# A row-wise infinity norm: new widths for the loads of the last eight tiles

## The chip, the cores and the metric

The kernel runs on one core of one Trainium2 chip. The metric is the device time of one execution in microseconds (us). All executions told of here are in the fast state, with a granted clock of 1.0; no other cores run.

Some terms. A partition is one of the 128 rows of the on-chip memory. VectorE is the engine that runs the reduces here; SyncE issues the loads (`nc.sync`), ScalarE's queue most of the stores (`nc.scalar`). A semaphore is a counter that a finished load raises and that a waiting instruction watches; a load has landed when its semaphore has reached its full count.

## The reference

```python
x = np.random.randn(8192, 8192).astype(np.float32)
def reference(x):
    return np.linalg.norm(x, ord=np.inf, axis=1)
```

For each row of 8192 numbers the result is the largest absolute value. The input is 268.4 MB, the output 32 KB, and each number is looked at once.

## The kernel before

Each of 128 partitions holds two rows in a tile of 16384 columns (64 KB a partition, 8 MB in all). Three such buffers are in use. The first 24 tiles, "the bulk", are loaded whole and reduced whole; the last eight, "the tail", are loaded in the pieces that `TAIL` lists, each row by itself, and each piece is reduced as it lands, so that little work is left after the last byte.

```python
TAIL = (
    [[8192]] * 8
    + [[4096, 4096]] * 5
    + [[2048] * 4] * 2
    + [[2048, 2048, 2048, 1024, 512, 512]]
)
# ... (cut: start_first_load_early, which moves the first load to the program's head; shapes)
    def absmax(o, i):
        nc.vector.reduce_max(out=o, in_=i, axis=X, apply_absolute_value=True)

    for a in range(A):              # bulk
        for n in range(G):
            t = sbuf.tile([P, B * cols + 16], F32, tag="t")
            nc.sync.dma_start(out=t[:, : B * cols], in_=x_b[a, n])
            absmax(r_bulk[:, a, n * B : (n + 1) * B],
                   t[:, : B * cols].rearrange("p (b c) -> p b c", b=B))
    nc.scalar.dma_start(out=out_b, in_=r_bulk[:])

    for i in range(0, n_tail, B):   # tail
        t = sbuf.tile([P, B * cols + 16], F32, tag="t")
        for j in range(B):
            r = i + j; at = j * cols; last = r == n_tail - 1
            for k, w in enumerate(TAIL[r]):
                nc.sync.dma_start(out=t[:, at : at + w], in_=x_t[i // B][:, at : at + w])
                if last and k == k_last - 1:
                    absmax(r_tail[:, : n_tail - 1], part[:])
                    nc.scalar.dma_start(out=out_t[:, : n_tail - 1], in_=r_tail[:, : n_tail - 1])
                    absmax(r_fin[:], t[:, at : B * cols + k_last - 1])
                elif last:          # partial results stand right behind the row
                    absmax(t[:, B * cols + k : B * cols + k + 1], t[:, at : at + w])
                else:
                    absmax(part[:, r, k : k + 1], t[:, at : at + w])
                at += w
    nc.sync.dma_start(out=out_t[:, n_tail - 1 :], in_=r_fin[:])
```

The last reduce of the last row reads the last piece together with the partial results behind it, so no further reduce is needed.

## Time and profile before

The time was 629.22 us (median of three executions, 629.04 to 629.8). The profiled one took 629.1, of which the profile's span holds 627.3.

| what | before |
|---|---|
| DMA share and throughput, 60 to 470 us | 1.00, 433 GB/s |
| VectorE busy | 552.7 us (88%) |
| last load lands | 622.73 us |
| last reduce ends | 624.96 us |
| result's store lands | 626.40 us |

The landing times come from the trace's record of each load, from its issue to the last increment of its semaphore. From the page of the kernel before: the span, the busy engines, groups of reduces (count, then busy time and mean ns of one, then idle time of VectorE ahead of them and what ended it), and the store of the bulk results (count, size, us from issue to landing).

```profile
span 627.3 us, 196 instructions
...
DVE 552.7 (88%) x58; POOL 0.2 (0%) x4
...
L81 DVE TENSOR_REDUCE r_bulk<-t 128x2 f32<-128x16384 f32 x24 | 413.3, 17220 | 69.7 <-DMA t<-in_x_dram 69.7
L81 DVE TENSOR_REDUCE part<-t 128x1 f32<-128x4096 f32 (+2 forms) x26 | 130.0, 5067 | 1.3 <-DMA t<-in_x_dram 1.3
L81 DVE TENSOR_REDUCE t<-t 128x1 f32<-128x2048 f32 (+2 forms) x5 | 8.6, 1746 | 0.3 <-DMA t<-in_x_dram 0.3
...
out_dram<-r_bulk ACTq DMA_DIRECT2D x1, 24.0 KB, 57.9
```

In the bulk VectorE waits 69.7 us for loads, and this costs nothing, since the loads are the limit. In the tail it waits 1.3 + 0.3 us.

From the table of stretches of the kernel before (stretch, its length, busy time of VectorE and of GpSimd, clock, DMA share, GB/s):

```profile
60.00:470.00 410.00, 364.90 (x22) 0.00 (x0) 1.00 1.00 433
...
600.00:622.00 22.00, 21.63 (x11) 0.00 (x0) 1.00 1.00 418
```

The DMA engines are full, nearly to the end. The Trainium skill, "DMA: Bandwidth & Descriptors", section "Specifications", gives 435 GB/s as the fabric's ceiling; this trace's 433 agrees with it. By these two figures another arrangement of the same bytes could shorten the middle by half a per cent at most.

From the timeline of the kernel before, the drain (start, duration, engine, instruction, count, and in brackets the idle time before it and what ended it):

```profile
617.75 2.29 DVE L81 TENSOR_REDUCE t<-t 128x1 f32<-128x2048 f32 x1 [0.15 <-DMA t<-in_x_dram]
620.23 4.00 DVE L81 TENSOR_REDUCE t<-t 128x1 f32<-128x2048 f32 x3 [0.19 <-DMA t<-in_x_dram]
624.26 0.69 DVE L81 TENSOR_REDUCE r_fin<-t 128x1 f32<-128x517 f32 x1
624.98 0.35 SPq L117 DMA_DIRECT2D out_dram<-r_fin  x1
```

The chain of waits of the kernel before ends in the same place:

```profile
603.13 17.07 DMA t<-in_x_dram
620.20 0.02 issue
620.23 2.55 DVE t L81 x2
...
624.26 0.69 DVE r_fin L81
```

At 620.20 the last load of 2048 columns lands and VectorE, which waited for it, starts its reduce. From there VectorE is never idle, and the end is fixed: the reduces of 2048, 1024, 512 and 512 columns one after the other. The last load lands meanwhile, at 622.73, and waits its turn. Between the last landing and VectorE's end lie 2.23 us, called the lag from here on.

From SyncE's queue of the kernel before, what it waited for (us in total, times, longest):

```profile
SPq L100 <- DMA out_dram<-r_bulk: 23.2, 1, 23.2
```

The program has eight completion semaphores for DMAs, used in turn, so a load waits for the DMA eight before it. One of those is the slow store of the bulk results.

### The profile page before, as it was taken

The numbers are of one execution on the slowest core, as the hardware profiler recorded it, in microseconds if no ns is written. First come the engines' busy times: TensorE is split into PE (matmuls) and PEld (weight loads), VectorE is DVE, ScalarE is ACT, GpSimd is POOL, SyncE is SP. The second block draws the span as 40 slices with busy tenths as digits, with TensorE's granted clock in tenths as the row PEclk, the third lists the DMA queues.
The fourth block names the chain that finished last, engine by engine and source line by source line (L and its number), as shares of the span: only waits on it lengthen the run. The fifth ranks groups of instructions, "written<-read, shape, count | busy, mean of one in ns | idle before, by whom it ended". The sixth has DMA issues, their size and how long they took to land.

```text
span 627.3 us, 196 instructions
## 1 busy us (share of the span) xinstructions
DVE 552.7 (88%) x58; POOL 0.2 (0%) x4
## 2 busy tenths in 40 slices
DVE  0588988889988889888898888998889999999998
POOL 0000000000000000000000000000000000000000
DMA  9999999999999999999999999999999999999996
GB/s 401 468 401 464 405 460 410 455 414 451 418 451 418 451 418 447 422 447 422 447 422 447 422 447 422 447 422 443 426 420 428 425 433 435 426 429 427 427 425 274
DMA packets 9138, 268.49 MB, mean 428 GB/s; under 512 B 1968, under 2 KB 1968, under 8 KB 2352
## 3 DMA queue, kind: packets, MB, share of 16 engines
q1 hardware_dynamic: 8208, 268.44, 99.2%
q10 hardware_dynamic: 928, 0.03, 0.1%
q14 instruction: 2, 0.02, 0.0%
HBM read 268.44 MB, written 0.03 MB: 428 GB/s over the span
## 4 chain that ended last, share of the span: by engine, by line
DMA 64%; DVE 30%; another core or an unknown queue 4%; issue 1%; SPq 0%
DMA t<-in_x_dram 64%; DVE r_bulk L81 24%; DVE part L81 5%; DVE t L81 1%; SPq L100 0%; DVE r_fin L81 0%
## 5 line engine op out<-in xcount | busy, mean ns | idle before, releaser
L81 DVE TENSOR_REDUCE r_bulk<-t 128x2 f32<-128x16384 f32 x24 | 413.3, 17220 | 69.7 <-DMA t<-in_x_dram 69.7
L81 DVE TENSOR_REDUCE part<-t 128x1 f32<-128x4096 f32 (+2 forms) x26 | 130.0, 5067 | 1.3 <-DMA t<-in_x_dram 1.3
L81 DVE TENSOR_REDUCE t<-t 128x1 f32<-128x2048 f32 (+2 forms) x5 | 8.6, 1746 | 0.3 <-DMA t<-in_x_dram 0.3
L78 DVE MEMSET part<- 128x60 f32 x1 | 0.1, 108 | 0.9 <-PEq L133 0.9
L81 DVE TENSOR_REDUCE r_fin<-t 128x1 f32<-128x517 f32 x1 | 0.7, 691 | 0.0
L81 DVE TENSOR_REDUCE r_tail<-part 128x15 f32<-128x60 f32 x1 | 0.2, 216 | 0.0
L133 POOL MEMSET const-bfloat16-1.0<- 128x1 bf16 x1 | 0.1, 101 | 0.0
L133 POOL MEMSET const-uint8-127<- 128x1 uint8 x1 | 0.1, 101 | 0.0
L133 POOL MEMSET const-float32-0.0<- 128x1 f32 x1 | 0.1, 98 | 0.2 <-issue 0.2
L133 POOL MEMSET const-float32-1.0<- 128x1 f32 x1 | 0.1, 98 | 0.0
## 6 DMA issues: line engine op xcount, KB each, us to landing
t<-in_x_dram SPq DMA_DIRECT2D x8, 4096.0 KB, 37.0
t<-in_x_dram SPq DMA_DIRECT2D x10, 2048.0 KB, 30.4
t<-in_x_dram SPq DMA_DIRECT2D x11, 1024.0 KB, 24.6
t<-in_x_dram SPq DMA_DIRECT2D x1, 512.0 KB, 15.9
t<-in_x_dram SPq DMA_DIRECT2D x2, 256.0 KB, 13.2
t<-in_x_dram SPq DMA_DIRECT2D x24, 40.7
out_dram<-r_bulk ACTq DMA_DIRECT2D x1, 24.0 KB, 57.9
out_dram<-r_tail ACTq DMA_DIRECT2D x1, 7.5 KB, 5.6
```

Of the source, the lines that this page charges most:

```text
L78: nc.vector.memset(part[:], 0.0)
L81: nc.vector.reduce_max(out=o, in_=i, axis=X, apply_absolute_value=True)
L133: nc = _bacc.Bacc("TRN2", target_bir_lowering=False, num_devices=1)
```

## The change

A reduce costs about 1.04 ns a column and a load about 1.18 ns, a ratio of 0.88. If each load has 0.88 of the width of the one before, each reduce is done about when the next load lands. The change writes the last two tiles about so, from 3968 down to 1024 columns with one step up (1024 to 1152). The change also lets a load cross from one row of a tile to the next; a reduce does not cross, so seven loads get two reduces. Loads in the tail go from 32 to 31, reduces of loaded columns from 32 to 38.

```diff
-TAIL = (
-    [[8192]] * 8
-    + [[4096, 4096]] * 5
-    + [[2048] * 4] * 2
-    + [[2048, 2048, 2048, 1024, 512, 512]]
-)
+TAIL = [
+    [2944, 13440],
+    [4096, 12288],
+    [11520, 4864],
+    [7680, 8704],
+    [6528, 3328, 6528],
+    [4864, 4096, 3328, 4096],
+    [3968, 3584, 3328, 2944, 2560],
+    [2432, 2176, 1920, 1664, 1536, 1280, 1152, 1024, 1152, 1024, 1024],
+]
+def segments(loads, cols):          # (load, row, column, width), cut at row ends
+    ...
@@ tail loop (cut) @@
+    for i, loads in enumerate(TAIL):
+        t = sbuf.tile([P, W + PAD], F32, tag="t")
+        for j, w in enumerate(loads):
+            nc.sync.dma_start(out=t[:, at : at + w], in_=x_t[i][:, at : at + w])
+            at += w
+            for _, b, c, n in [s for s in todo if s[0] == j]:
+                ...                 # one absmax for each segment, results as before
```

The store of the first 15 tail rows now stands in the program right after the last reduce of row 15, no longer behind the last load. In the kernel before, too, it was issued at that point (at 615.44 us).

More of the change, by code (lines that the diff above doesn't have):

```diff
@@ L13 @@
 X = mybir.AxisListType.X
-TAIL = (
-    [[8192]] * 8
-    + [[4096, 4096]] * 5
-    + [[2048] * 4] * 2
-    + [[2048, 2048, 2048, 1024, 512, 512]]
-)
+TAIL = [
[9 more added lines that the diff above has]
+def segments(loads, cols):
+    out, at = [], 0
+    for i, w in enumerate(loads):
+        end = at + w
+        while at < end:
+            r = at // cols
+            to = min(end, (r + 1) * cols)
+            out.append((i, r, at - r * cols, to - at))
+            at = to
+    return out
 def start_first_load_early(nc):
@@ L51 @@
     BUFS: int = 3,
+    PAD: int = 16,
 ):
@@ L55 @@
     rows, cols = x.shape
-    n_tail = len(TAIL)
-    assert n_tail % B == 0
+    W = B * cols
+    n_tail = B * len(TAIL)
     n_bulk_rows = rows // P - n_tail
@@ L70 @@
     outp = ctx.enter_context(tc.tile_pool(name="outp", bufs=1))
-    k_last = len(TAIL[-1])
+    segs = [segments(loads, cols) for loads in TAIL]
+    count = {}
+    for i, s in enumerate(segs):
+        for _, r, _, _ in s:
+            count[i * B + r] = count.get(i * B + r, 0) + 1
+    n_last = count[n_tail - 1]
+    k_max = max(count[r] for r in range(n_tail - 1))
+    assert n_last - 1 <= PAD
     r_bulk = outp.tile([P, A, G * B], F32)
@@ L75 @@
     r_fin = outp.tile([P, 1], F32)
-    k_max = max(len(r) for r in TAIL[:-1])
     part = outp.tile([P, n_tail - 1, k_max], F32)
@@ L84 @@
         for n in range(G):
-            t = sbuf.tile([P, B * cols + 16], F32, tag="t")
-            nc.sync.dma_start(out=t[:, : B * cols], in_=x_b[a, n])
+            t = sbuf.tile([P, W + PAD], F32, tag="t")
+            nc.sync.dma_start(out=t[:, :W], in_=x_b[a, n])
             absmax(
                 r_bulk[:, a, n * B : (n + 1) * B],
-                t[:, : B * cols].rearrange("p (b c) -> p b c", b=B),
+                t[:, :W].rearrange("p (b c) -> p b c", b=B),
             )
     nc.scalar.dma_start(out=out_b, in_=r_bulk[:])
-    for i in range(0, n_tail, B):
-        t = sbuf.tile([P, B * cols + 16], F32, tag="t")
-        for j in range(B):
-            r = i + j
-            at = j * cols
-            last = r == n_tail - 1
-            for k, w in enumerate(TAIL[r]):
-                nc.sync.dma_start(
-                    out=t[:, at : at + w], in_=x_t[i // B][:, at : at + w]
-                )
-                if last and k == k_last - 1:
-                    absmax(r_tail[:, : n_tail - 1], part[:])
-                    nc.scalar.dma_start(
-                        out=out_t[:, : n_tail - 1], in_=r_tail[:, : n_tail - 1]
-                    )
-                    absmax(r_fin[:], t[:, at : B * cols + k_last - 1])
-                elif last:
-                    absmax(
-                        t[:, B * cols + k : B * cols + k + 1], t[:, at : at + w]
-                    )
-                else:
-                    absmax(part[:, r, k : k + 1], t[:, at : at + w])
-                at += w
@@ new lines @@
+    seen = {}
+    for i, loads in enumerate(TAIL):
+        t = sbuf.tile([P, W + PAD], F32, tag="t")
+        todo = segs[i]
+        at = 0
+        for j, w in enumerate(loads):
+            nc.sync.dma_start(out=t[:, at : at + w], in_=x_t[i][:, at : at + w])
+            at += w
+            for _, b, c, n in [s for s in todo if s[0] == j]:
+                r = i * B + b
+                k = seen.get(r, 0)
+                seen[r] = k + 1
+                lo = b * cols + c
+                if r < n_tail - 1:
+                    absmax(part[:, r, k : k + 1], t[:, lo : lo + n])
+                    if r == n_tail - 2 and k == count[r] - 1:
+                        absmax(r_tail[:, : n_tail - 1], part[:])
+                        nc.scalar.dma_start(
+                            out=out_t[:, : n_tail - 1], in_=r_tail[:, : n_tail - 1]
+                        )
+                elif k < n_last - 1:
+                    absmax(t[:, W + k : W + k + 1], t[:, lo : lo + n])
+                else:
+                    absmax(r_fin[:], t[:, lo : W + n_last - 1])
```

## The prediction

> **What bounds the kernel.** The loads. From 60 to 470 us the stretch table shows a DMA share of 1.00 and 433 GB/s; the Trainium skill, "DMA: Bandwidth & Descriptors", section "Specifications", gives 435 GB/s as the fabric ceiling, so nothing is left there, and the 268.4 MB stay the same. VectorE is 88% busy (page, part 1). In the bulk a 16384-column tile lands every 19.34 us and its reduce takes 17.22 us (timeline); some 20 us of loads are outstanding at each issue, so the queue never runs dry.
>
> Open are only the start (first landing 22.0 us, untouched) and the drain. In the trace the last load lands at 622.73 us, the last reduce ends at 624.95, its store lands at 626.40, and the span ends at 627.32 (the measured time adds 1.9). Only the 2.2 us between last landing and VectorE's end are for sale.
>
> **Why 2.2 us.** Reduces cost about 1.04 ns a column plus 0.06 us (starts 8.59 us apart for 8192 columns, 2.20 for 2048, 1.13 for 1024); loads 1.18 ns a column. VectorE enters the tail 17.2 us behind and gains 2.2 us a tile, so it has little to spare: it idles 1.67 us in the tail (timeline: 0.38, 0.56, 0.38, 0.15, 0.19). The last wait is at 620.20, for a load of 2048; its reduce (2.2 us) then stands in front of 1024, 512 and 512, which land within 2.5 us. A step of a half is too steep for rates that differ by 12%.
>
> **What the change does.** Loads 32 -> 31, reduces 32 -> 38 (row boundaries split seven loads): +0.4 us of VectorE work. Each load is about 0.88 of the one before, so a reduce ends about when the next load lands, and the backlog shrinks to that of one 1024-column load. Replaying the tail with these two rates gives 624.85 for the present kernel (trace: 624.95) and 623.9 for the changed one: waits of 0.9 us near 505 and 519 us, none after, and a last reduce of 1.2 us that starts as the last load lands. Both bounds agree: last landing + 1.25 = 624.0; VectorE's tail work without waits from 483.85 = 623.7. Gain 0.9 us, all at the chain's end.
>
> **What could take it back.** Eight completion semaphores serve in turn, so a load can wait for the DMA eight before. The bulk results' store takes 57.9 us (page, part 6): its 48 small packets per engine alternate with big load packets (same page, "Queues, rings and completion order": round robin at packet granularity; 57.9/48 = 1.21 us, one 32 KB packet, agrees). SyncE waits 23.2 us for it (its queue's waits). The first four tail tiles still have two loads each, so again 48 load packets pass; it should land at 542 and release the second load of tail tile 5 while earlier loads cover it to 551. If the store gets an earlier semaphore, loads could starve 1 to 3 us. Small loads cost some 0.03 us each.
>
> **Predicted.** 628.3 us, 8 in 10 between 627.6 and 629.4. Faster by over 2%: 0.005; within 2%: 0.975; slower by over 2%: 0.02.
>
> **Signs.** Right: last landing at 622.5 to 623.0; last reduce of 1030 columns, 1.2 us, starting within 0.2 us of it; DMA share 1.00 through the tail; no VectorE wait over 0.5 us after 545. Wrong: a dip in GB/s near 540 to 550 (starvation); a last reduce starting over 0.5 us after the last landing (backlog; splits dearer than 0.06 us); last landing after 623.3 (small loads dearer).
>
> **What would make it wrong.** Another order of semaphores, or a cost of widths that are no powers of two.

## The result, and the profile after

The changed kernel took 628.45 us (median of six executions, 628.34 to 629.09), the kernel before 629.20 (six, 629.04 to 629.8). The ratio is 0.9988, with a 95% interval of 0.9975 to 1.0001. Ratios are the mean time of one kernel's fast runs over that of the other's of the same rounds, so not quite the ratio of the medians. In three later rounds of five executions each the changed kernel was again faster: medians 0.97, 1.07 and 0.68 us under the kernel before. So the change is worth 0.7 to 1.1 us of 629, about a seventh of a per cent, and within 2%. Of the four intervals two lie under 1 throughout (a0 and a1 below) and two just reach it (1.0001 and 1.0003); it is the fourfold repetition that makes the sign clear.

From the page of the changed kernel:

```profile
span 627.3 us, 201 instructions
...
DVE 553.0 (88%) x64; POOL 0.2 (0%) x4
...
L106 DVE TENSOR_REDUCE r_bulk<-t 128x2 f32<-128x16384 f32 x24 | 413.3, 17220 | 70.1 <-DMA t<-in_x_dram 70.1
L106 DVE TENSOR_REDUCE part<-t 128x1 f32<-128x8192 f32 (+18 forms) x31 | 130.5, 4273 | 0.9 <-DMA t<-in_x_dram 0.6
L106 DVE TENSOR_REDUCE t<-t 128x1 f32<-128x1152 f32 (+3 forms) x6 | 7.9, 1387 | 0.0
```

The two spans are equal, 627.3 us. This pair of profiles alone would say that nothing was gained. But the profiled execution of the changed kernel was the slowest of its six (629.09 us), and it lost 0.4 us in the bulk, which the change does not touch: the last bulk tile landed at 467.13 us against 466.69. The parts say more than the whole. VectorE's work grew by 0.3 us, the six further reduces, and its waits in the tail shrank from 1.6 us to 0.9.

From the timeline and from the chain of waits of the changed kernel:

```profile
519.67 96.02 DVE L106 TENSOR_REDUCE part<-t 128x1 f32<-128x8192 f32 x25 [0.64 <-DMA t<-in_x_dram]
...
615.86 7.90 DVE L106 TENSOR_REDUCE t<-t 128x1 f32<-128x1536 f32 x6
...
623.80 1.23 DVE L106 TENSOR_REDUCE r_fin<-t 128x1 f32<-128x1030 f32 x1
625.05 0.35 SPq L144 DMA_DIRECT2D out_dram<-r_fin  x1
```

```profile
598.15 17.56 DVE part L106 x7
...
615.94 7.83 DVE t L106 x6
623.77 0.02 issue
623.80 1.23 DVE r_fin L106
```

No bracket after 519.67 (the view shows idle times from 0.15 us): VectorE hardly waits for a load any more, and the chain that ended last runs on VectorE alone for its last 27 us. The last load landed at 623.60 and the last reduce began 0.20 us later; the lag is 1.43 us in place of 2.23.

From the table of stretches and SyncE's waits of the changed kernel, the same places as before:

```profile
60.00:470.00 410.00, 364.47 (x22) 0.00 (x0) 1.00 1.00 433
...
600.00:622.00 22.00, 21.97 (x13) 0.00 (x0) 1.00 1.01 422
```

```profile
SPq L124 <- DMA out_dram<-r_bulk: 25.1, 1, 25.1
```

For all kernels the table gives, from one profile each: the time from the last bulk tile's landing to the last landing (how long the loads of the tail took), the lag, and their sum, which takes the noise of the bulk out.

| kernel | tail loads, us | lag, us | sum, us | last wait of VectorE, us | 8 KB instruction fetches after 400 us, at us |
|---|---|---|---|---|---|
| before | 156.04 | 2.23 | 158.27 | 620.2 | 587.6, 626.2 |
| after, 4 profiles | 156.47, 156.52, 156.26, 156.53 | 1.43, 1.43, 1.42, 1.43 | 157.90, 157.95, 157.69, 157.96 | 597 | 578.2 to 578.8, 592.7 to 593.3 |
| last tile only | 156.22 | 1.72 | 157.94 | 593.6 | 587.4, 624.4 |
| first seven only | 156.27 | 2.21 | 158.49 | 620.4 | 578.6, 592.4 |
| short last reduce | 155.98 | 0.40 | 156.38 | 520.3 | 579.5, 593.5 |
| ends in 512 | 156.74 | 1.48 | 158.22 | 597.2 | 578.5, 592.9 |
| store by slab | 156.46 | 1.44 | 157.91 | 597.2 | 578.4, 592.9 |
| no row splits | 156.19 | 1.56 | 157.75 | 588.9 | 587.6, 625.7 |
| control, old widths | 156.01 | 2.23 | 158.24 | 620.1 | 587.6, 626.1 |
| old widths, padded | 156.42 | 2.20 | 158.62 | 620.7 | 567.9, 588.5 |
| one tail store | 156.08 | 1.51 | 157.59 | 519.3 | 578.5, 592.7 |

### The profile page after: what moved, and what is told of

The parts are those of the page before. It is cut to its first block, busy times and chain, and to the rows that moved or that the text cites. A ratio compares the mean times of both kernels' runs of the same rounds, so it can differ in the third digit from the quotient of the medians.

```text
span 627.3 us, 201 instructions
## 1 busy us (share of the span) xinstructions
DVE 553.0 (88%) x64; POOL 0.2 (0%) x4
## 4 chain that ended last, share of the span: by engine, by line
DMA 67%; DVE 28%; another core or an unknown queue 4%; SPq 0%; issue 0%
DMA t<-in_x_dram 67%; DVE r_bulk L106 22%; DVE part L106 5%; DVE t L106 1%; DVE r_fin L106 0%; SPq L124 0%; DVE r_tail L106 0%
## 5 line engine op out<-in xcount | busy, mean ns | idle before, releaser
L106 DVE TENSOR_REDUCE part<-t 128x1 f32<-128x8192 f32 (+18 forms) x31 | 130.5, 4273 | 0.9 <-DMA t<-in_x_dram 0.6
L106 DVE TENSOR_REDUCE t<-t 128x1 f32<-128x1152 f32 (+3 forms) x6 | 7.9, 1387 | 0.0
```

## The experiments

Four theories were in play. D, the drain: the gain is the shorter lag, and the lag is set by VectorE's last wait and by the work that it has after it. L, the loads: the new widths make the loads themselves faster. W: only the width of the last loads matters. F, which came up on reading the trace of the changed kernel: its longer VectorE program brings one more instruction fetch into the stretch of the loads and holds them up. Smaller rivals are told where they belong. Each experiment is an edit of the changed kernel and was timed in five rounds beside the kernel before; all results were found correct by the comparison with the reference (one with a reservation, told below). The second round (a1 to e6) ran on another chip than the first and the third.

| run | median, us | range, us | before in the same rounds: median, range, us | ratio |
|---|---|---|---|---|
| a0_after_again | 628.67 | 628.49 to 628.81 | 629.64, 629.35 to 630.09 | 0.9984 |
| e1_last_tile_only | 629.49 | 629.09 to 630.13 | the same | 0.9997 |
| e2_first_seven_only | 629.24 | 629.12 to 630.03 | the same | 0.9995 |
| e3_short_last_reduce | 627.77 | 627.68 to 628.30 | the same | 0.9970 |
| a1_after_third | 628.74 | 628.62 to 629.47 | 629.81, 629.11 to 629.96 | 0.9987 |
| e4_end_512 | 629.39 | 629.21 to 629.59 | the same | 0.9995 |
| e5_store_by_slab | 628.93 | 628.53 to 629.52 | the same | 0.9987 |
| e6_no_row_splits | 629.15 | 628.64 to 629.67 | the same | 0.9991 |
| a2_after_fourth | 628.48 | 628.37 to 628.92 | 629.16, 629.09 to 629.84 | 0.9989 |
| c0_old_widths | 629.25 | 629.03 to 629.37 | the same | 1.0000 |
| e7_old_widths_padded | 629.51 | 629.38 to 630.05 | the same | 1.0005 |
| e8_one_tail_store | 628.55 | 628.38 to 629.38 | the same | 0.9993 |

The 95% interval of each ratio reaches 0.0012 to 0.0014 to each side, 0.8 us. Under 1 throughout lie those of a0, a1 and e3 alone, so the traces carry more of the argument than the times.

### The yardsticks and a control

The changed kernel went along in each of three rounds, without an edit.

> The changed kernel again, as the yardstick of this round. Theory D (drain: the gain is the shorter backlog between the last landing and the end of VectorE): 0.7 to 0.9 us under the kernel before, with the last reduce ending 1.2 to 1.5 us after the last landing (before: 2.2). Rival L (loads: the new widths make the loads themselves land earlier): last landing 0.7 us or more earlier than before, and the distance from last landing to the end of VectorE unimportant.

> The changed kernel once more, as the yardstick of this round: 0.7 to 1.0 us under the kernel before. In its trace two instruction fetches of 8 KB (on the instruction queue) at about 578 and 593 us, as in both earlier traces of it, and the load that lands next after the first of them about 0.5 us late.

> The changed kernel as the yardstick of this round: 0.7 to 1.0 us under the kernel before.

Measured: 0.97, 1.07 and 0.68 us under the kernel before. Its lag was 1.43, 1.42 and 1.43 us, and the reduction from 2.23 is the same in every profile. Against L: the tail's loads did not get faster, they took 0.2 to 0.5 us longer than before (156.26 to 156.53 against 156.04).

The control is the changed program text with the old widths:

```diff
-    [2944, 13440], ... (the new eight lists)
+    [8192, 8192], [8192, 8192], [8192, 8192], [8192, 8192],
+    [4096, 4096, 4096, 4096], [4096, 4096, 4096, 4096],
+    [4096, 4096, 2048, 2048, 2048, 2048],
+    [2048, 2048, 2048, 2048, 2048, 2048, 2048, 1024, 512, 512],
```

> A control: the changed program text, with the old widths. It issues the loads and reduces of the kernel before, so every theory expects its time, within 0.2 us; what it differs by is the noise of such a comparison.

Measured: 629.25 us against 629.16, and in the table above no number of its trace differs from that of before by more than 0.1 us. The program text is not the cause; the widths are. Here two medians of one and the same work differ by 0.09 us. But the kernel before moved from round to round (medians 629.64, 629.81 and 629.16), the changed kernel less (628.67, 628.74 and 628.48), so the comparison with the changed kernel of the same round is the better one.

### One half of the change at a time

The new widths in the last tile alone, the old ones in the seven before it:

```diff
-    [2944, 13440], ... (first seven lists)
+    (first seven lists of the control)
     [2432, 2176, 1920, 1664, 1536, 1280, 1152, 1024, 1152, 1024, 1024],
```

> Only the last tail tile has the new widths; the first seven have the old ones. Theory D with a VectorE work budget (VectorE comes into the last tile with the old kernel's backlog, and the waits of the first seven, about 1.6 us, are not won back): a replay with 1.18 ns a loaded column and 1.04 ns plus 0.06 us a reduce gives VectorE's end 0.5 us earlier than before, so about half of the gain, -0.5 us, and a last reduce that starts about 0.4 us after the last landing. Rival W (only the width of the last loads matters, the first seven tiles are decoration): the whole gain, -0.8 us. Rival L: some gain in proportion to the columns changed, an eighth, -0.1 us.

And the other way round:

```diff
     [2944, 13440], ... (first seven lists)
-    [2432, 2176, 1920, 1664, 1536, 1280, 1152, 1024, 1152, 1024, 1024],
+    [2048, 2048, 2048, 2048, 2048, 2048, 2048, 1024, 512, 512],
```

> The first seven tail tiles have the new widths; the last has the old ones. Theory D: VectorE's last wait is again for a 2048-column load with 1024, 512 and 512 behind it, so the end is as before: 0.0 to -0.1 us. Rival L: most of the gain, -0.7 us, since seven eighths of the changed columns are here.

Measured, in the traces: with the last tile alone the lag is 1.72 us, and the last reduce starts 0.49 us after the last landing (0.4 expected). With the first seven alone the lag is 2.21 us, as before. The timeline of the second shows why: VectorE again waits for the last load of 2048 columns, and the rest is the old drain.

```profile
620.38 4.01 DVE L106 TENSOR_REDUCE t<-t 128x1 f32<-128x2048 f32 x3 [0.20 <-DMA t<-in_x_dram]
624.42 0.69 DVE L106 TENSOR_REDUCE r_fin<-t 128x1 f32<-128x517 f32 x1
```

Both lags are what D expected. The times are less clear. Against the changed kernel of the same round the two lose 0.82 and 0.57 us, so neither half brings the whole gain; that is against W, which gave it all to the last tile, and against L, which gave most of it to the first seven. But they cannot place the halves between nothing and 0.5 us: the last tile alone was expected 0.5 us under the kernel before and its median was 0.15 under, with a spread of 1 us; its fastest two executions (629.09, 629.13) are 0.2 to 0.3 under the fastest of before (629.35). By the sum in the table its one profile is as good as the changed kernel's (157.94), with one fetch less among the loads, of which more below. That size is open.

### Take away the last reduce

The last reduce reads only the last 64 columns and the scratch values. The result of one row of each partition may be wrong: 960 of its 8192 columns are skipped, so by chance some 15 of these 128 maxima lie there (an estimate). The comparison with the reference did not notice it.

```diff
-                    absmax(r_fin[:], t[:, lo : W + n_last - 1])
+                    absmax(r_fin[:], t[:, W - 64 : W + n_last - 1])
```

> The changed kernel, whose last reduce reads only the last 64 columns and the scratch values (the result of that one row of each partition is wrong on purpose). It takes nothing from the loads. Theory D: the last reduce of 1.23 us becomes about 0.2 us, and the whole difference shows in the time: 1.0 us under the changed kernel, about 1.8 us under the kernel before. Rival L, or an end that hangs on the loads or the last store's queue: no more than 0.2 us under the changed kernel.

Measured: 627.77 us, 0.90 us under the changed kernel of the same round and 1.87 under the kernel before. The timeline of this run:

```profile
616.02 7.90 DVE L106 TENSOR_REDUCE t<-t 128x1 f32<-128x1536 f32 x6
...
623.96 0.23 DVE L106 TENSOR_REDUCE r_fin<-t 128x1 f32<-128x70 f32 x1
624.21 0.35 SPq L144 DMA_DIRECT2D out_dram<-r_fin  x1
```

The reduce fell from 1.23 to 0.23 us, the lag from 1.43 to 0.40, and nearly all of the 1.0 us shows in the time. This is the clearest of the experiments: no load was touched, and a microsecond taken from VectorE's end is a microsecond of the kernel. It is theory D, and against L. (In this profile the loads were also spared the delay by an instruction fetch that is told of below; the lag does not depend on it.)

### A finer end

If a last load of 1024 is better than the old drain, is one of 512 better still?

```diff
-    [2432, 2176, 1920, 1664, 1536, 1280, 1152, 1024, 1152, 1024, 1024],
+    [2432, 2176, 1920, 1664, 1472, 1280, 1088, 960, 896, 832, 640, 512, 512],
```

> The changed kernel with a finer last row: 1472, 1280, 1088, 960, 896, 832, 640, 512, 512 in place of 1536 to 1024, 1024, so two more loads and reduces and a last reduce of 0.7 us. Theory D with a VectorE budget (VectorE has no wait left near the end that a smaller load could use, so smaller loads only move the backlog and add 0.06 us each): the last reduce starts 0.5 to 0.7 us after the last landing instead of 0.05 to 0.2, VectorE still ends 1.2 to 1.4 us after the last landing, time as the changed kernel, within 0.2 us. Rival W (the width of the last load sets the end): VectorE ends about 0.75 us after the last landing, time 0.5 us under the changed kernel.

Measured: 629.39 us, 0.65 us slower than the changed kernel of the same round. The lag did not fall (1.48 us, 1.2 to 1.4 expected), which is what D with a VectorE budget says and W does not; the time, which D expected within 0.2 us of the changed kernel, is a miss for both. In the timeline of this run the last reduce is short, but it starts late:

```profile
615.71 8.56 DVE L106 TENSOR_REDUCE t<-t 128x1 f32<-128x1472 f32 x8
...
624.30 0.69 DVE L106 TENSOR_REDUCE r_fin<-t 128x1 f32<-128x520 f32 x1
```

It started 0.78 us after the last landing (623.52); without a wait since 597.2 us, VectorE had simply not got there. Two more reduces added about 0.1 us of work. The loads, too, took longer, 156.74 us. Of that, 0.24 us came at 544 us, where no width was changed, so the finer end is not its cause, and the profile does not explain all of the 0.65 us. No gain from a finer end is shown; a loss of that size is measured and only partly explained.

### Take away the wait for the slow store

SyncE's wait of 25 us for the bulk results' store was the risk named in the prediction. The prediction took from the Trainium skill, "DMA: Bandwidth & Descriptors", section "Queues, rings and completion order", that a DMA engine serves its queue rows in turn, packet by packet; so 48 small packets an engine wait for 48 large ones. If the results go out slab by slab within the bulk, only 8 packets an engine are left in the tail.

```diff
                 t[:, :W].rearrange("p (b c) -> p b c", b=B),
             )
-    nc.scalar.dma_start(out=out_b, in_=r_bulk[:])
+        nc.scalar.dma_start(out=out_b[:, a : a + 1], in_=r_bulk[:, a : a + 1])
```

> The changed kernel, with the bulk results stored slab by slab inside the bulk (six stores of 8 packets an engine in place of one of 48), so that SyncE's wait of 25 us for that store at 519 to 544 us goes. Theory D (loads queued ahead cover that wait): the time stays within 0.2 us of the changed kernel, and the throughput near 545 us is what it was. Rival S (the blocked loads and the burst of issues after it cost something, for instance the 0.5 us lost near 580 us): 0.3 to 0.6 us under the changed kernel, and the late landing near 580 us gone.

Measured: the wait is gone from SyncE's list. The six stores took 23.4 us each (median), a packet an engine about every 2.4 us, beside the large packets of the bulk (64 KB), and eight packets at 19.34 / 8 = 2.42 us (a bulk tile's time over its eight packets an engine) are 19.3 us, most of it; so the account of alternating packets holds in this run as well. The time, 628.93 us, is 0.19 us over the changed kernel of the same round, inside the expected 0.2. The late landing near 584 us is still there. So the wait cost nothing: at 544.54 us, when the store landed, loads issued earlier still covered 8 us (the 6528 columns issued at 519 landed at 552.58). Rival S falls.

### Fewer reduces

The record of the changed kernel showed the last load of the sixth tail tile (4096 columns) landing at 584.27 us, 0.54 us later than its width allows. In the three repetitions it was 0.59, 0.38 and 0.63 late. Just before it, at 578 us, a fetch of 8 KB on the instruction queue took 0.31 us, and by the trace's packet records a load packet that started as the fetch ended took twice its normal time (16 KB, 1.24 us). Theory F says that VectorE's longer program brings this fetch. With the old widths in six tiles no load crosses a row, and there are 32 reduces again:

```diff
-    [2944, 13440], ... (first seven lists)
+    [8192, 8192], [8192, 8192], [8192, 8192], [8192, 8192],
+    [4096, 4096, 4096, 4096], [4096, 4096, 4096, 4096],
+    [4352, 3840, 3072, 2688, 2432],
     [2432, 2176, 1920, 1664, 1536, 1280, 1152, 1024, 1152, 1024, 1024],
```

> The last tail tile as in the changed kernel; the six before it as in the kernel before, and 4352, 3840, 3072, 2688, 2432 in the one between: 32 reduces as before in place of 38, since no load crosses a row. Theory D: a replay with the same rates gives VectorE's end at 1.3 us after the last landing, as in the changed kernel, although it waits 1.4 us in the tail in place of 0.9; so the gain over the kernel before stays 0.7 us or more. Theory F (VectorE's longer program brings a second instruction fetch into the tail, which holds up a load and with it the last landing by about 0.4 us): only one fetch left in the tail, the last landing 156.0 to 156.2 us after the last bulk tile's in place of 156.5, and the time 0.2 to 0.4 us under the changed kernel. Without F: as the changed kernel, within 0.1 us.

Measured, in the trace: one fetch less among the loads (the other moved behind the end, to 625.7 us), the tail's loads in 156.19 us as F expected, the lag 1.56 us. In the time: 629.15 us, 0.41 over the changed kernel of the same round where 0.2 to 0.4 under it was expected. The five executions range over 1.0 us, and the profiled one was the fastest of them (628.64). So F was right about the fetch and about the landing (though 156.19 also lies among the tails with two fetches, 155.98 to 156.74, so the landing alone decides little), and its expected gain in time is a miss. D's gain of 0.7 us or more over the kernel before was just missed as well (0.66 by the medians, and a lag of 1.56 where 1.3 was expected).

### Bring the fetch in, and change nothing else

The control with old widths, plus eight tiny instructions at the start, where VectorE waits 21 us anyway:

```diff
     nc.vector.memset(part[:], 0.0)
+    for _ in range(8):
+        nc.vector.memset(r_fin[:], 0.0)
```

> The control with eight tiny memsets more at VectorE's start, where it waits 21 us for the first tile. No instruction of the tail changes; VectorE's program only becomes as long as that of the changed kernel. Theory F (a longer VectorE program brings one more instruction fetch into the stretch of the loads, and the DMA engine that serves it is late with its share of the loads): an 8 KB fetch between 480 and 600 us that the control lacks, the last landing 0.2 to 0.5 us later after the last bulk tile, and the time 0.2 to 0.4 us over the control. Rival: no such fetch, or a fetch that costs nothing; time within 0.1 us of the control.

Measured: 629.51 us against 629.25 for the control, 0.26 more by the medians and 0.35 by the means. The DMA queues between 480 and 600 us (packets, MB, share of the time of 16 engines), first of the control, then of the padded kernel:

```profile
q14 instruction: 1, 0.01, 0.0%
```

```profile
q14 instruction: 2, 0.02, 0.0%
```

The further fetch came at 567.9 us; the load that landed next, at 569.3, was 0.47 us late, and the tail's loads took 156.42 us in place of 156.01. The lag did not change (2.20 against 2.23), so the lateness went into the end. Every execution of the padded kernel (629.38 us and up) lies above every one of the control (629.37 and down). With the old widths, then, theory F is shown, by one profile of each kernel and five times of each: nothing in the tail was edited. The Trainium skill, same page and section, lists the queue row 14 as internal to the runtime and names "refill" among its uses, which agrees with the name of the queue here; what one costs that page does not say.

How a fetch delays a load, and why by different amounts, can be read from the packets and semaphores of the traces. In every profile here a load packet that starts as a fetch among the loads ends takes 0.41 to 0.66 us longer than its neighbours. But a load has landed only with the last of its semaphore's sixteen increments, which are taken here for its share on each of the 16 DMA engines (the trace does not name the engine). In the padded kernel's loads after the fetch the last increment comes 0.34 to 0.47 us behind the one before it, to the end; in the control from 568 us on never more than 0.11. One late engine, then, makes all loads after it late. With the short last reduce the last increment was already 1.04 us behind the one before it when the fetch came. The fetch made another late (the second-last now stood 0.45 us before the last), no more than that, and the landing was 0.05 us late. A fetch costs the landing only as far as its engine becomes the last one.

In the changed kernel, too, this reaches the end. Seven profiles have the same loads in the tail and the same reduces up to the last one: the four of the changed kernel, the short last reduce, the store by slab and the one tail store. All have the fetch near 578 us. After it the next load was late by 0.05 us (short last reduce), 0.27 (one tail store) and 0.38 to 0.66 (the others), and the last reduce started 156.15, 156.36 and 156.46 to 156.74 us after the last bulk tile's landing. So nearly the whole lateness comes out at VectorE's end. The waits that the profile lists after the fetch (0.12 and 0.10 us in the first profile, at 589.04 and 597.33) are a little under half of it. The rest is lost overlap: reduces that need not wait overlap by about 0.08 us (at 4096 columns in the kernel before: 4.41 us long, starts 4.33 apart), and one that must wait does not.

### One store for the tail

```diff
-                        nc.scalar.dma_start(
-                            out=out_t[:, : n_tail - 1], in_=r_tail[:, : n_tail - 1]
-                        )
-                    absmax(r_fin[:], t[:, lo : W + n_last - 1])
-    nc.sync.dma_start(out=out_t[:, n_tail - 1 :], in_=r_fin[:])
+                    absmax(r_tail[:, n_tail - 1 :], t[:, lo : W + n_last - 1])
+    nc.sync.dma_start(out=out_t, in_=r_tail[:])
```

> The changed kernel with the results of the tail stored once, at the end, in place of 15 of 16 columns about 8 us before it and one at the end. Theory D: the end is last landing, last reduce, one store; the early store was off the chain, so the time stays within 0.2 us of the changed kernel, and the last store takes 1.4 us as before although it is larger. Rival P (the early store's packets hold up the last loads): the loads after 615 us land 0.1 to 0.3 us earlier, and the time falls by as much.

Measured: 628.55 us against 628.48 for the changed kernel of the same round: no difference. The final store took 1.4 us with 16 columns as with one. The early store was off the chain, as D has it; P falls. No kernel that computes every row beat the changed one.

## Why the prediction was right

- **The time.** 628.3 us was predicted, 628.45 measured; a gain of 0.9 us, and 0.75 in the first comparison, 0.68 to 1.07 in the others. That the two times agree to 0.15 us is in part luck: the kernel before alone moved by 0.65 us between rounds (medians 629.16 to 629.81), and a delay that the prediction did not know of was at work (below).
- **What is for sale.** Only the 2.2 us between last landing and VectorE's end, said the prediction. The short last reduce shows it: 1.0 us taken from there gave 0.90 us, with the loads as they were.
- **The lag.** Predicted 1.25 us, measured 1.42 or 1.43 in all four profiles. The rest is that the last reduce had to wait 0.20 us for VectorE itself.
- **The price of the splits.** Predicted +0.4 us of VectorE's work; the page says 552.7 to 553.0 us.
- **The waits.** Predicted 0.9 us in the tail with the larger one near 519 us and none over 0.5 us after 545; measured 0.9 us (page), 0.64 us at 519.67, and none over 0.12 after 545.
- **What could take it back.** The store's wait was predicted harmless, and the run without it agrees; the sign of starvation, a dip near 540 to 550 us, did not come (435 GB/s from 530 to 560). Its landing was predicted at 542 us and came at 544.54; the store took 60.1 us, not 57.9.
- **Where it was off: the steps.** "Each load is about 0.88 of the one before" holds for the last two tiles, not for the six before. These matter less: with the old widths there (the run without row splits) the lag was 1.56 us, against 2.23 before and 1.43 with the change (its time decides nothing).
- **Where it was off: the last landing.** Predicted 622.5 to 623.0 us, with "after 623.3" as a sign of dear small loads. It came at 623.60 in the first profile and at 623.15 to 623.24 in the repetitions. 0.44 us of the first was bulk noise. The other 0.2 to 0.5 us is not what the sign was to tell: the lateness sits at one load of 4096 columns near 584 us, right after an instruction fetch, which the prediction had not thought of; the padded kernel shows such a fetch to cost 0.4 us of landing with the old widths. That the new widths themselves cost nothing is shown by the short last reduce: the same loads, with the fetch on an engine that was not the last, took 155.98 us (before: 156.04).
- **What stays open.** By the profiles, last bulk tile to VectorE's end, the changed kernel gained 0.3 to 0.6 us (158.27 and 158.24 against 157.69 to 157.96). By the medians it gained 0.68 to 1.07 us. The fetch accounts for the profiles: its four cost 0.4 to 0.6 us of landing. Where it cost none, with the short last reduce, the last reduce started at 156.15 us; with 1.23 us for a whole one the sum would be 157.38 (an estimate), 0.89 under the kernel before, which is the predicted gain of 0.9. Why the medians gained more than the profiles is open. The profiled execution of the changed kernel was the slowest or second slowest of its set each time, that of the control the fastest of its five, so a lateness that differs from execution to execution can do this, but no run shows that it does. The times of the two halves, and of the kernel without row splits, are open for the same reason.

## What to carry to other kernels

When a kernel streams at the DMA's limit and its compute engine is only a little faster (here 12%), the backlog shrinks slowly, and the end is decided by the last time that the compute engine waits: everything that it must do after that wait stands behind it. Let the pieces shrink by about the ratio of the two rates, and do not expect more from still finer ones: the finer end brought nothing here. Shown is this for one kernel and one ratio. For effects under 1 us compare the stretch that was changed, not the span, since the streaming part alone moved by up to 1.2 us from profile to profile (last bulk tile at 466.63 to 467.81 us), and count the instructions that were added: here they brought a fetch that took back up to 0.6 us of the gain in the profiles.

## What the Trainium skill lacked or had wrong

- "DMA: Bandwidth & Descriptors" names row 14 as the runtime's own, with "refill", but gives no cost; instruction fetches are treated in "Runtime: NRT & Kernel Launch", section "Instruction fetch mechanics", which does not say what one does to the loads beside it. Here an 8 KB fetch on that queue took 0.31 us and made the next load packet 0.41 to 0.66 us longer. With nothing else changed in the tail it delayed the last landing by 0.41 us (156.42 against 156.01) and the kernel by about 0.3 us; where its engine was not the last, it delayed the landing by 0.05. With 58 or 59 reduces and memsets on VectorE there was one such fetch among the loads (587 us), with 63 or more there were two.
- "DMA: Bandwidth & Descriptors" gives a DMA a fixed cost of about 2 us and a part that grows with its bytes, measured for DMAs that GpSimd issues (section "Anatomy of one DMA — SWDGE (gpsimd) path"). The stores here are issued by ScalarE, so that fit is not tested. A store of 24 KB in 32-byte packets took 57.9 us, and one of 4 KB 23.4 us; 48 turns with a 32 KB load packet and eight with one of 64 KB give 58 and 19 us of it. The rule of taking turns stands on that page; that a store is slowed by the packet size of the loads beside it does not.
- Where "DMA: Bandwidth & Descriptors" gives 435 GB/s for the fabric and about 358 for HBM for each core, this run, on one core, held 433 GB/s from HBM for 410 us; the page's note on single-core numbers allows it.
